# Projections with the split activations side by side as one moving operand, and a prologue by channel tiles

## The chip, the cores and the metric

The kernel runs on one core of a Trainium2 chip. Five engines share the work: TensorE (PE in the profile; its weight loads are listed apart as PEld), VectorE (DVE), ScalarE (ACT), GpSimd (POOL) and SyncE (SP), which issues most transfers from memory. Each engine executes its own queue in order; engines wait for each other on semaphores. The metric is the device time of one execution in microseconds (us). Several executions are timed, and the median counts.

## The reference

A trunk of two layers works on 256 tokens of 1024 channels, in float32. Each layer is, cut to what matters:

```python
h = rms_norm(x, norm_mix_pre)
proj = h @ w_in                      # 1024 -> 1536 + 4*512 + 32 + 512 + 3*1024
u_hy, q, k, v, g_out, gate_lr, u_pool, gate_logits = split(proj)
y_hy   = hyena(u_hy)                 # conv3, then a long convolution by FFT with a filter made by a sine MLP
y_gla  = gla(q, k, v, g_out, gate_lr)  # gated linear attention, 4 heads, both directions
y_pool = pool(u_pool)                # centred means over 2, 4, 8, 16 tokens, 128x128 product per group
gates  = sigmoid(gate_logits)        # 3 x 1024
merged = gates0 * (y_hy @ w_br_hyena) + gates1 * (y_gla @ w_br_gla) + gates2 * (y_pool @ w_br_pool)
x = x + rms_norm(merged @ w_out, norm_mix_post)
h = rms_norm(x, norm_ffn_pre)
a, b = split(h @ ffn_w_up)           # 2 x 2816
y = (gelu(conv3(a)) * b) @ ffn_w_down
x = x + rms_norm(y, norm_ffn_post)
```

## The kernel before

All large products are done in a reduced-precision float format (float32r) by three terms: each operand is split into an upper part (rounded, written by ACT) and a lower part (the rest, a subtraction on DVE), and the product is upper x upper + upper x lower + lower x upper, added up in PSUM. The helper `split` does this for activations, `mm3` issues the three products.

Weights come in chunks of 1 MB (128 partitions x 2048), 71 per layer, through three `raw` buffers that SP's queue fills (`dma_next`). `split_half` splits half a chunk: one ACT instruction (128x1024) and one DVE subtraction. A `unit` is one step of PE's work: it makes sure that its chunk is split, issues its products, runs the pending evictions of earlier units, and then, for each 2.6 us of PE cost, calls `tick` (each running side job, such as the Hyena, attention and pooling jobs, issues its next step) and one or two `filler` splits of later chunks. `ahead` says how many chunks ahead the fillers may go. Between the windows opened by `open_window`, in which PE, DVE and ACT keep the written order, a planner orders the instructions of each engine by priority and a simulated timeline.

Buffers are taken from three pools: `big` (37 of 4 KB per partition), `sml` (9 of 2 KB) and `psm` (8 PSUM banks of 2 KB, 512 columns each). Side jobs wait in `tick` until enough are free (`len(psm.free) < 3`, `len(sml.free) < 3`).

The normalised activations are transposed so that channels lie on partitions: `xt` holds 8 channel tiles (k = 0 to 7) of 256 tokens. Before the change, it is four `big` buffers: two for the upper parts and two for the lower parts, with four channel tiles each. `transposes` fills them from two PSUM banks, one half of the channels at a time.

Two forms of projection use `xt`. `chunk_x_stationary` loads a piece of x as the stationary operand and streams 512 weight columns past it (values and output gates of the attention, branch gates, the output projection, and the first 1024 columns of the b half of the up projection). `two_ftiles` loads weights and streams the 256 tokens: it makes two tiles of 128 output channels (f = 0, 1) in the two halves of one PSUM bank, by two units of 24 products, 256 columns each. Its `post` reads the bank. In a layer's mixer there are 12 calls: eight channel-pair projections whose post is `hy_post` (a conv3 per tile, on ACT and then twice on DVE) or `qk_post` (two DVE instructions of 128x512), in the order x1, v, x1, v, x0, x0, q, q, then two `pool_post` (a copy by ACT, then a side job), then two for k. The up projection has 18 calls: 11 for a (`a_post`: conv3 for both tiles, then gelu on ACT) and 7 for b (`b_post`: a multiplication, and the split for the down projection). The mixer of layer 0 also hosts that layer's filter job (`filt`); the filter of layer 1 runs within the up projections of layer 0.

The prologue is written out by hand. x is loaded in three transfers (two halves of the first 128 tokens, then the second 128), with the first weight chunk between them in two transfers of 512 KB; `grow`, the first norm's gains, goes on SP's queue ahead of the weights. `squares(t)` gives the sums for row tile t on ACT and DVE, `scaled` multiplies by the reciprocal root, `turned` transposes on PE into four PSUM banks, `gained(t, half, ps, banks)` applies the gains and splits. `upper(k)` and `lower(k)` split a quarter of the first chunk. The second row tile's transposes are issued by `second` from within the first unit.

Of the kernel before, what the change touches and what calls it, by code (L numbers as in the profile page):

```python
# [18 lines left out]
P = 128  # L19
# [62 lines left out]


@with_exitstack
def trunk(ctx: ExitStack, tc: tile.TileContext, a: dict, out: bass.AP):
# [5 lines left out]
    big = Slots(spool, "b", 37, 4096)  # L91
    sml = Slots(spool, "s", 9, 2048)
    psm = Slots(ppool, "p", 8, 2048)
# [76 lines left out]
    grow = cpool.tile([8, P], F32, name="grow")  # L170
    nc.sync.dma_start(grow[:], a["gains"][0, 0].rearrange("(k c) -> k c", c=P))

# [10 lines left out]
    def dma_next(parts=1, between=None):  # L183
        n = state["dma"]
        if n >= len(order):
            return
        kind, c = order[n]
        w = 2048 if kind == "w" else 512
        r = wpool.tile([P, w], F32, tag="raw", name=f"raw{n}")
        src = a["wts"][c] if kind == "w" else a["lrw"][c]  # L190
        if kind == "w" and c % NCHUNK in PAIRED:
            side = (c % NCHUNK - 16) % 3
            for m in range(2):
                src = a["wts"][c - side + m][:, side * 1024:(side + 1) * 1024].rearrange("p (k c) -> p k c", c=256)
                nc.sync.dma_start(r[:].rearrange("p (k c) -> p k c", c=512)[:, :, m * 256:(m + 1) * 256], src)
            parts = 0
        for m in range(parts):
            s = slice(m * w // parts, (m + 1) * w // parts)
            nc.sync.dma_start(r[:, s], src[:, s])
            if between is not None and m == 0:  # L200
                between()
        raws[n] = r
        state["dma"] = n + 1
# [50 lines left out]

    dma_next(2, lambda: load_x(1, [slice(0, DM)]))
    dma_next(2)
# [112 lines left out]
    def transposes(h, t, xth, xtl):  # L369
# [7 lines left out]
        for half in range(2):  # L377
            split(xth[half][:, :, s], xtl[half][:, :, s], ps[half][:])
        psm.put(*ps)
# [87 lines left out]
    def filt(i, kf):  # L467
# [102 lines left out]
    def ftile(n, xt, f, o, width=256, kn=8):  # L570
        xth, xtl = xt
        for k in range(kn):
            h, l = weights(n, k * width + f * P, P)
            mm3(o, h, l, xth[k // 4][:, k % 4, :], xtl[k // 4][:, k % 4, :], k == 0, k == kn - 1)

    def two_ftiles(n, xt, post):
        ps = psm.get([P, 2, L])
        unit([n], lambda: ftile(n, xt, 0, ps[:, 0, :]))

        def fin():  # L580
            post(ps)
            psm.put(ps)

        unit([n], lambda: ftile(n, xt, 1, ps[:, 1, :]), fin, free=n)

# [5 lines left out]
    def layer(i, xt, chains):  # L591
# [152 lines left out]

        two_ftiles(take(), xt, hy_post("x1", 0))
        two_ftiles(take(), xt, hy_post("v", 0))
        two_ftiles(take(), xt, hy_post("x1", 2))
        two_ftiles(take(), xt, hy_post("v", 2))

# [137 lines left out]
        x0 = room([P, 4, L])  # L887
        two_ftiles(take(), xt, hy_post("x0", 0))
        f_hy = start(hyena())
        two_ftiles(take(), xt, hy_post("x0", 2))  # L890

# [3 lines left out]
        big.put(g2)  # L895
        two_ftiles(take(), xt, qk_post(eb, 0, float(P ** -0.5)))
        handles["x0"] = True
        two_ftiles(take(), xt, qk_post(eb, 1, float(P ** -0.5)))

# [64 lines left out]

        two_ftiles(take(), xt, pool_post(0))
        two_ftiles(take(), xt, pool_post(2))
        for pair in range(2):
            two_ftiles(take(), xt, qk_post(enb, pair, None))

# [96 lines left out]
        def branch(b, ready):  # L1066
            for half in range(2):
# [15 lines left out]
                if b == 2 and half == 1:  # L1083
                    flush()
                    big.put(*xt[0], *xt[1])
                if b == 2:
# [52 lines left out]
        for t in range(2):  # L1139
            banks = [psm.get([P, 512]) for _ in range(2)]  # L1140
            ready = [False, False]
            ch2.append(start(post_norm(t, banks, g_post_t, g_pre2, *xt2, ready), LIFT))
            for c in range(4):
# [101 lines left out]
        for at, (t, c) in enumerate(seq):  # L1245
            if not done_first and c == 1:
                done_first = True
                flush()
                big.put(*xt2[0], *xt2[1])
                xt3 = xt_alloc() if not last else (None, None)  # L1250

            def fin(t=t):
                ch3.append(start(post_norm(t, banks[t], g_post2, None if last else g_cur["pre"], *xt3), LIFT))
            oldest = min(cc for _, cc in seq[at:])
# [5 lines left out]
        if last:  # L1260
            ready = [False, False]
            ch3.append(start(post_norm(1, banks[1], g_post2, None, *xt3, ready)))
            tail = [(half, c) for half in range(2) for c in range(11 - LEAD, 11)]
# [243 lines left out]
```

## Time and profile before

| what | value |
|---|---|
| time, median of 3 runs | 886.82 us (885.36 to 887.30) |
| profiled execution, its own time | 885.61 us |
| its span, first to last instruction | 883.8 us |
| granted TensorE clock | 0.998 of full speed |
| PE busy | 871.4 us, 5381 products |
| DVE busy | 635.8 us, 925 instructions |
| ACT busy | 511.8 us, 809 instructions |
| memory traffic | 163.46 MB, mean 185 GB/s |

The profiled execution is one run with the hardware profiler on; its own time is a little longer than the span, which begins at the first instruction and ends with the last. Busy time is the time in which an engine had at least one instruction in work. Lines such as L120 or L111 are helpers that record all products or all DVE subtractions, so instructions are told apart by their tiles: `b<-raw,b` is the lower part of a weight split, `p<-b,b` a product of two large buffers, `s<-p` a read of a PSUM bank into a small buffer. In a row of a timeline the columns are start and length in us, engine, line, operation, tiles, shapes, count, and in brackets the idle time before and what ended it.

### The profile page before, as it was taken

The page shows a single profiled execution, that of the slowest core. Times are in us where ns is not written, and L with a number is a line of the kernel's source. Part 1 is how long each engine was busy: PE and PEld are TensorE (multiplying, and loading weights), DVE is VectorE, ACT ScalarE, POOL GpSimd, SP SyncE. Part 2 cuts the span into 40 slices and gives each one's busy share as a digit, 9 for nine tenths or more (in the row PEclk, how much of TensorE's full clock was granted, in tenths as well). Part 3 has the DMA queues.
Part 4 walks back from the last instruction along what each step waited for, and adds up shares of the span by engine and source line. Part 5 has one row for each costly group of instructions (what it writes and reads, how often), then busy time and mean ns, then how long its engine had stood idle before and what let it go on. Part 6 is the DMA issues. An engine that isn't in the chain of part 4 may idle for free.

```text
span 883.8 us, 13488 instructions
## 1 busy us (share of the span) xinstructions
PE 871.4 (99%) x5381; PEld 782.4 (89%) x5381; DVE 635.8 (72%) x925; ACT 511.8 (58%) x809; POOL 37.9 (4%) x86
## 2 busy tenths in 40 slices
PE   8999999999999999999999999999999999999996
PEld 6899987888888999998889999888888899999885
DVE  6899989766586798665288989876755967776612
ACT  6778757555365776554267855864543665555501
POOL 3000100000010000000010000000000000000000
PEclk9999999999999999999999999999999999999999
DMA  8863625746546436466349453455752674455501
GB/s 287 325 233 131 215 96 190 240 145 238 191 159 246 143 134 248 149 221 224 121 136 349 161 164 131 153 195 179 279 184 78 239 281 144 168 170 207 195 1 48
DMA packets 48143, 163.46 MB, mean 185 GB/s; under 512 B 3410, under 2 KB 29157, under 8 KB 33232
## 3 DMA queue, kind: packets, MB, share of 16 engines
q1 hardware_dynamic: 44080, 151.70, 48.9%
q0 software_dynamic: 4000, 10.90, 3.8%
q8 instruction: 42, 0.69, 0.3%
q14 instruction: 21, 0.17, 0.1%
HBM read 161.54 MB, written 1.05 MB: 184 GB/s over the span
## 4 chain that ended last, share of the span: by engine, by line
PE 95%; DVE 2%; DMA 1%; ACT 1%; issue 0%; SPq 0%; DVEq 0%; POOLq 0%; ACTq 0%
PE p L120 93%; DMA raw<-in_wts 1%; DVE b L111 1%; ACT b L106 1%; PE p L374 1%; PE p L1059 0%; PE p L1204 0%; PE p L775 0%; PE p L1021 0%; PE p L876 0%; DVE s L111 0%; PE p L1294 0%; SPq L159 0%; DVE x L114 0%; DVEq L1503 0%
## 5 line engine op out<-in xcount | busy, mean ns | idle before, releaser
L120 PE MATMUL p<-b,b 128*128 128x256 f32 (+2 forms) x5022 | 840.1, 328 | 4.0 <-DVE b L111 2.3
L120 PEld LDWEIGHTS p<-b,b 128*128 128x128 f32 x5022 | 739.8, 190 | 86.6 <-DVE b L111 3.7
L111 DVE TENSOR_TENSOR b<-raw,b 128x1024 fp32r<-128x1024 f32 (+2 forms) x288 | 342.3, 1208 | 114.1 <-ACT b L106 59.6
L106 ACT ACTIVATE b<-raw 128x1024 fp32r<-128x1024 f32 (+2 forms) x290 | 292.2, 1041 | 161.2 <-PE p L120 127.4
L111 DVE TENSOR_TENSOR b<-p,b 128x512 f32<-128x512 f32 (+2 forms) x72 | 45.8, 655 | 66.1 <-ACT s L106 44.6
L106 ACT ACTIVATE b<-p 128x512 f32<-128x512 f32 (+3 forms) x90 | 50.0, 571 | 64.2 <-PE p L120 38.7
L106 ACT ACTIVATE s<-p 128x256 f32<-128x256 f32 (+3 forms) x50 | 20.3, 415 | 69.0 <-PE p L120 68.7
L114 DVE SCALAR_TENSOR_TENSOR s<-p,vec,s 128x255 f32<-128x255 f32 x104 | 49.4, 479 | 6.5 <-ACT s L106 5.5
L106 ACT ACTIVATE s<-p,vec 128x256 f32<-128x256 f32 x52 | 28.8, 557 | 18.1 <-DVE s L114 15.5
L106 ACT ACTIVATE s<-s 128x512 f32<-128x512 f32 (+6 forms) x54 | 28.9, 535 | 11.5 <-DVE s L111 5.6
L111 DVE TENSOR_TENSOR b<-s,b 128x512 fp32r<-128x512 f32 (+1 forms) x42 | 28.6, 686 | 6.0 <-ACT b L106 6.0
L106 ACT ACTIVATE b<-s 128x512 fp32r<-128x512 f32 x38 | 23.5, 625 | 9.2 <-DVE s L111 9.1
L111 DVE TENSOR_TENSOR b<-b,b 128x512 f32<-128x512 f32 (+4 forms) x28 | 22.4, 802 | 3.6 <-ACT b L106 3.1
L111 DVE TENSOR_TENSOR b<-b,p 128x512 f32<-128x512 f32 x24 | 16.2, 683 | 7.7 <-PE p L120 7.3
L111 DVE TENSOR_TENSOR s<-s,p 128x512 f32<-128x512 f32 x22 | 15.0, 684 | 8.4 <-ACT s L106 8.0
L106 ACT ACTIVATE b<-b,s 128x128 f32<-128x128 f32 x64 | 20.5, 392 | 0.4 <-DVE s L700 0.4
L114 DVE SCALAR_TENSOR_TENSOR b<-p,vec,b 128x255 f32<-128x255 f32 (+1 forms) x40 | 19.1, 478 | 0.4 <-ACT b L106 0.3
L387 POOL TENSOR_TENSOR rstd<-mse,mhalf 128x1 f32<-128x1 f32 x16 | 9.3, 581 | 210.5 <-DVE mse L117 210.5
L106 ACT ACTIVATE b<-p,vec 128x256 f32<-128x256 f32 (+1 forms) x24 | 12.6, 527 | 9.0 <-PE p L120 7.1
L106 ACT ACTIVATE b<-b 1x512 f32<-1x512 f32 (+3 forms) x16 | 12.5, 783 | 4.2 <-DVE b L111 4.1
L106 ACT ACTIVATE s<-x 128x512 f32<-128x512 f32 x12 | 7.6, 634 | 11.6 <-DVE x L114 11.4
L111 DVE TENSOR_TENSOR s<-b,b 128x512 f32<-128x512 f32 x20 | 13.1, 685 | 1.5 <-PE p L120 1.4
(108 smaller groups left out, 310.7 us busy)
## 6 DMA issues: line engine op xcount, KB each, us to landing
raw<-in_wts SPq DMA_DIRECT2D x116, 1024.0 KB, 4.8
raw<-in_wts SPq DMA_DIRECT2D x52, 512.0 KB, 5.3
b<-in_gains POOLq DMA_DIRECT2D x7, 512.0 KB, 4.5
b<-in_dft POOLq DMA_DIRECT2D x4, 512.0 KB, 6.9
b<-in_gw POOLq DMA_DIRECT2D x2, 512.0 KB, 5.5
b<-in_fw POOLq DMA_DIRECT2D x2, 512.0 KB, 7.3
b<-in_decay POOLq DMA_DIRECT2D x2, 512.0 KB, 7.3
out<-x SPq DMA_DIRECT2D x4, 256.0 KB, 2.0
```

The lines of the kernel that those rows point to most:

```text
L106: ins = nc.scalar.activation(o, i, func, **kw)
L111: nc.vector.tensor_tensor(out=o, in0=x, in1=y, op=op)
L114: nc.vector.scalar_tensor_tensor(out=o, in0=x, scalar=s, in1=y, op0=op0, op1=op1)
L120: ins = nc.tensor.matmul(o, w, x, start=start, stop=stop).ins
L374: nc.tensor.transpose(ps[k // 4][:, k % 4, :], h[:, k * P:(k + 1) * P], ident[:])
L387: nc.gpsimd.tensor_tensor(out=r[:], in0=e[:], in1=mhalf[:, 0:1], op=ALU.pow)
```

## The change

Five things change.

1. `xt` is laid out by channel tiles: four buffers, each with two channel tiles, and for each of them the upper part and then the lower part, 512 columns in a row. `Part` gives the old view of it (upper or lower part of a channel tile), so that other users are the same. `transposes` writes each half of the channels in two pieces.
2. `two_ftiles` has a wide form, used in layer 1's mixer (`i > 0`) and in both layers' up projections. It takes one small buffer and two banks, one bank for each of the two output tiles. A first unit issues, for both tiles, 8 products each of the upper weights with 512 columns (upper x into the bank's first half, lower x into its second half); a second unit issues 8 products each of the lower weights with the 256 columns of the upper x, into the first half. Then ACT copies the second half to the small buffer and DVE adds the first half to it, for each tile, and `post` reads the small buffer in place of a PSUM bank. The costs that the units give are 3.6 and 1.9 in place of 2.6 and 2.6.
3. `sml` has 10 buffers.
4. In the prologue, the first weight chunk comes in four transfers, with x's second row tile after two of them; `grow` is issued from ACT's queue; `squares(1)` goes ahead of the second part of `gained(0, 0, ...)`, and `scaled(1, ...)` ahead of `lower(3)`.
5. In the filter job, the upper part of the last filter weight (`w3h`) is issued on ACT behind `hs`, the upper part of the sines.

```diff
+class Part:
+    def __init__(self, tiles, m):
+        self.tiles, self.m = tiles, m
+    def __getitem__(self, at):
+        _, k, s = at
+        return self.tiles[k // 2][:, k % 2, self.m, s]
+    def two(self, j, s):
+        return self.tiles[j][:, :, self.m, s]
...
-    sml = Slots(spool, "s", 9, 2048)
+    sml = Slots(spool, "s", 10, 2048)
...
-    nc.sync.dma_start(grow[:], a["gains"][0, 0].rearrange("(k c) -> k c", c=P))
+    nc.scalar.dma_start(grow[:], a["gains"][0, 0].rearrange("(k c) -> k c", c=P))
...
-            if between is not None and m == 0:
+            if between is not None and 2 * m + 2 == parts:
...
-    dma_next(2, lambda: load_x(1, [slice(0, DM)]))
+    dma_next(4, lambda: load_x(1, [slice(0, DM)]))
...
         for half in range(2):
-            split(xth[half][:, :, s], xtl[half][:, :, s], ps[half][:])
+            for j in range(2):
+                split(xth[half].two(j, s), xtl[half].two(j, s), ps[half][:, 2 * j:2 * j + 2, :])
...
-        act(hs[:], h2[:])
+        with tc.issue_after(nc.scalar.activation(hs[:], h2[:], AF.Copy).ins):
+            act(w3h[:], kf["w3"][:])
         tt(hs[64:P, :], h2[64:P, :], f32(hs[64:P, :]), ALU.subtract)
-        act(w3h[:], kf["w3"][:])
         tt(w3l[:], kf["w3"][:], f32(w3h[:]), ALU.subtract)
...
     def xt_alloc():
-        return ([big.get([P, 4, L], F32R) for _ in range(2)], [big.get([P, 4, L], F32R) for _ in range(2)])
+        ts = [big.get([P, 2, 2, L], F32R) for _ in range(4)]
+        return (*([Part(ts[2 * j:2 * j + 2], m) for j in range(2)] for m in range(2)), ts)
...
+    def ftiles_wide(n, xt, banks, lows):
+        for f, o in enumerate(banks):
+            for k in range(8):
+                h, l = weights(n, k * 256 + f * P, P)
+                x = xt[2][k // 2][:, k % 2]
+                if lows:
+                    mm(o[:, 0, :], l, x[:, 0, :], False, k == 7)
+                else:
+                    mm(o[:], h, x, k == 0, False)
...
-    def two_ftiles(n, xt, post):
+    def two_ftiles(n, xt, post, wide=True):
+        if not wide:
...
+        while not sml.free:
+            tick()
...
+        tmp = sml.get([P, 2, L])
+        banks = [psm.get([P, 2, L]) for _ in range(2)]
+        def fin():
+            for f, ps in enumerate(banks):
+                act(tmp[:, f, :], ps[:, 1, :])
+                tt(tmp[:, f, :], tmp[:, f, :], ps[:, 0, :], ALU.add)
+            psm.put(*banks)
+            post(tmp)
+            sml.put(tmp)
+        unit([n], lambda: ftiles_wide(n, xt, banks, False), cost=3.6)
+        unit([n], lambda: ftiles_wide(n, xt, banks, True), fin, cost=1.9, free=n)
...
-        two_ftiles(take(), xt, hy_post("x1", 0))
+        two_ftiles(take(), xt, hy_post("x1", 0), i > 0)
...
     lower(1)
-    gained(0, 0, ps0, (1,))
     h1, ss1 = squares(1)
     r1 = rstd_mean(ss1)
-    for k in (2, 3):
-        upper(k)
-        lower(k)
+    gained(0, 0, ps0, (1,))
+    upper(2)
+    lower(2)
+    upper(3)
     scaled(1, h1, r1)
+    lower(3)
```

All 12 calls of `two_ftiles` in the mixer get `i > 0`; the calls of the up projections are left as they are written, so they take the wide form.

More of the change, by code (lines that the diff above doesn't have):

```diff
@@ L570, in ftile @@
     def ftile(n, xt, f, o, width=256, kn=8):
-        xth, xtl = xt
+        xth, xtl = xt[:2]
         for k in range(kn):
             h, l = weights(n, k * width + f * P, P)
-            mm3(o, h, l, xth[k // 4][:, k % 4, :], xtl[k // 4][:, k % 4, :], k == 0, k == kn - 1)
-    def two_ftiles(n, xt, post):
-        ps = psm.get([P, 2, L])
-        unit([n], lambda: ftile(n, xt, 0, ps[:, 0, :]))
-        def fin():
-            post(ps)
-            psm.put(ps)
-        unit([n], lambda: ftile(n, xt, 1, ps[:, 1, :]), fin, free=n)
+            s = slice(0, L)
+            mm3(o, h, l, xth[k // 4][:, k % 4, s], xtl[k // 4][:, k % 4, s], k == 0, k == kn - 1)
+    def ftiles_wide(n, xt, banks, lows):
[9 more added lines that the diff above has]
+        if not wide:
+            ps = psm.get([P, 2, L])
+            unit([n], lambda: ftile(n, xt, 0, ps[:, 0, :]))
+            def fin():
+                post(ps)
+                psm.put(ps)
+            unit([n], lambda: ftile(n, xt, 1, ps[:, 1, :]), fin, free=n)
+            return
+        c = 0
+        while not sml.free:
+            tick()
+            c += 1
+            assert c < 500, "no room"
+        tmp = sml.get([P, 2, L])
+        banks = [psm.get([P, 2, L]) for _ in range(2)]
+        def fin():
+            for f, ps in enumerate(banks):
[6 more added lines that the diff above has]
+        unit([n], lambda: ftiles_wide(n, xt, banks, True), fin, cost=1.9, free=n)
     def conv3(o, ps, i, col):
@@ L743, in hy_post @@
             return post
-        two_ftiles(take(), xt, hy_post("x1", 0))
-        two_ftiles(take(), xt, hy_post("v", 0))
-        two_ftiles(take(), xt, hy_post("x1", 2))
-        two_ftiles(take(), xt, hy_post("v", 2))
+        two_ftiles(take(), xt, hy_post("x1", 0), i > 0)
+        two_ftiles(take(), xt, hy_post("v", 0), i > 0)
+        two_ftiles(take(), xt, hy_post("x1", 2), i > 0)
+        two_ftiles(take(), xt, hy_post("v", 2), i > 0)
         def qk_post(dst, pair, scale):
@@ L887, in layer @@
         x0 = room([P, 4, L])
-        two_ftiles(take(), xt, hy_post("x0", 0))
+        two_ftiles(take(), xt, hy_post("x0", 0), i > 0)
         f_hy = start(hyena())
-        two_ftiles(take(), xt, hy_post("x0", 2))
+        two_ftiles(take(), xt, hy_post("x0", 2), i > 0)
         drain(f_dec, *gates_ready)
@@ L895, in layer @@
         big.put(g2)
-        two_ftiles(take(), xt, qk_post(eb, 0, float(P ** -0.5)))
+        two_ftiles(take(), xt, qk_post(eb, 0, float(P ** -0.5)), i > 0)
         handles["x0"] = True
-        two_ftiles(take(), xt, qk_post(eb, 1, float(P ** -0.5)))
+        two_ftiles(take(), xt, qk_post(eb, 1, float(P ** -0.5)), i > 0)
         pw = sml.get([P, 4, P])
@@ L963, in pool_post @@
             return post
-        two_ftiles(take(), xt, pool_post(0))
-        two_ftiles(take(), xt, pool_post(2))
+        two_ftiles(take(), xt, pool_post(0), i > 0)
+        two_ftiles(take(), xt, pool_post(2), i > 0)
         for pair in range(2):
-            two_ftiles(take(), xt, qk_post(enb, pair, None))
+            two_ftiles(take(), xt, qk_post(enb, pair, None), i > 0)
         y_gl = {}
@@ L1084, in branch @@
                     flush()
-                    big.put(*xt[0], *xt[1])
+                    big.put(*xt[2])
                 if b == 2:
@@ L1141, in layer @@
             ready = [False, False]
-            ch2.append(start(post_norm(t, banks, g_post_t, g_pre2, *xt2, ready), LIFT))
+            ch2.append(start(post_norm(t, banks, g_post_t, g_pre2, *xt2[:2], ready), LIFT))
             for c in range(4):
@@ L1248, in layer @@
                 flush()
-                big.put(*xt2[0], *xt2[1])
+                big.put(*xt2[2])
                 xt3 = xt_alloc() if not last else (None, None)
             def fin(t=t):
-                ch3.append(start(post_norm(t, banks[t], g_post2, None if last else g_cur["pre"], *xt3), LIFT))
+                ch3.append(start(post_norm(t, banks[t], g_post2, None if last else g_cur["pre"], *xt3[:2]), LIFT))
             oldest = min(cc for _, cc in seq[at:])
@@ L1261, in layer @@
             ready = [False, False]
-            ch3.append(start(post_norm(1, banks[1], g_post2, None, *xt3, ready)))
+            ch3.append(start(post_norm(1, banks[1], g_post2, None, *xt3[:2], ready)))
             tail = [(half, c) for half in range(2) for c in range(11 - LEAD, 11)]
```

## The prediction

> **What bounds the kernel now.** I read the page first, then who waited for whom on PE, then the stages.
>
> ```profile
> span 883.8 us, 13488 instructions
> PE 871.4 (99%) x5381; PEld 782.4 (89%) x5381; DVE 635.8 (72%) x925; ACT 511.8 (58%) x809; POOL 37.9 (4%) x86
> PE 95%; DVE 2%; DMA 1%; ACT 1%; issue 0%; SPq 0%; DVEq 0%; POOLq 0%; ACTq 0%
> ```
>
> ```profile
> PE p L120 <- DVE b L111: 2.3, 2, 1.8
> PE p L120 <- ACT b L106: 1.8, 2, 1.4
> ```
>
> PE is busy 99% of the span, is 95% of the chain that ended last, and its longest wait on another engine is 1.8 us. A busy PE is not a PE at its peak, so the rate comes from the chain in order of time (start, length, what). Two rows hold products of a single kind: 48 products of 512 columns between two sets of transposes, and 144 of 256 columns (three pairs of up projections).
>
> ```profile
> 254.18 10.90 PE p L120 x48
> ...
> 735.62 17.28 PE p L120 x144
> ```
>
> 10.90/48 = 0.2271 us per 512-column product, 17.28/144 = 0.1200 us per 256-column one. The 256 extra columns cost 0.1071 us, so 0.013 us of each product does not depend on its width. Each has its own weight load in both stages (PE and PEld both count 5381). So the time is the number of PE instructions and their columns, and fewer instructions for the same columns shorten it, unless DVE or ACT come late. Where that could be is in the stages (length, busy time of each engine, clock):
>
> ```profile
> 60.00:91.00 31.00, 31.00 (x246) 30.02 (x245) 30.90 (x63) 26.60 (x55) 1.87 (x6) 1.00 0.31 121
> 91.00:116.00 25.00, 25.00 (x199) 24.46 (x199) 22.63 (x39) 15.59 (x35) 2.51 (x8) 1.00 0.59 190
> 269.50:386.00 116.50, 116.50 (x904) 112.26 (x903) 89.01 (x129) 70.86 (x96) 2.68 (x5) 1.00 0.53 189
> 477.00:552.00 75.00, 75.00 (x615) 74.43 (x614) 65.75 (x118) 49.82 (x99) 3.81 (x13) 1.00 0.52 175
> 552.00:570.00 18.00, 18.00 (x92) 15.19 (x91) 16.63 (x28) 15.93 (x26) 0.00 (x0) 1.00 0.37 110
> 701.60:817.00 115.40, 115.40 (x925) 113.59 (x925) 80.31 (x104) 66.12 (x86) 0.57 (x1) 1.00 0.55 195
> ```
>
> Layer 0's mixer (60 to 116) has DVE at 30.90 of 31 us, and behind it stands the one long PE stall of the trace, 1.78 us before this row:
>
> ```profile
> 136.41 5.96 PE L120 MATMUL p<-b,b 128*128 128x512 f32 x25 [1.78 <-DVE b L111]
> ```
>
> The change leaves that mixer narrow. Layer 1's mixer (477 to 552) has DVE at 65.75 of 75; the up projections (269.5 to 386 and 701.6 to 817) at 89.01 of 116.5 and 80.31 of 115.4.
>
> **The change, part by part.** Wide products. A narrow two_ftiles is 2 x 8 x 3 = 48 products of 256 columns: 48 x 0.1200 = 5.76 us. A wide one is 16 of 512 and 16 of 256: 16 x 0.2271 + 16 x 0.1200 = 5.55 us. The gain is 0.206 us per call. Calls: 18 in layer 0's up projections, 12 in layer 1's mixer, 18 in its up projections, 48 in all: 3.7 + 2.5 + 3.7 = 9.9 us, and 768 PE instructions fewer. The wide row is taken from a stage that streams weights past x, but what counts is columns and one load per product, and these are the same.
>
> The Trainium skill, "TensorE: Matmul & The Clock Gate", section "Back-to-back issue gap", speaks against this: it gives N/2.4 + 2.5 ns between warm products, so only 2.5 ns of each would be saved, an estimate of 768 x 2.5 ns = 1.9 us in place of 9.9. The two rows above differ from it (120 ns for its 109, 227 for its 216), at a granted clock of 1.00, so the measured 13 ns decides.
>
> What a wide call adds, from groups with shapes kept apart (busy, mean ns of one):
>
> ```profile
> L106 ACT ACTIVATE s<-p 128x256 f32<-128x256 f32 (+3 forms) x50 | 20.3, 415 | 69.0 <-PE p L120 68.7
> L106 ACT ACTIVATE s<-p 128x256 f32<-128x256 f32 x16 | 5.8, 383 | 3.8 <-PE p L120 3.6
> L111 DVE TENSOR_TENSOR b<-p,b 128x256 fp32r<-128x256 f32 x8 | 3.4, 421 | 5.4 <-ACT b L106 5.4
> L114 DVE SCALAR_TENSOR_TENSOR s<-p,vec,s 128x255 f32<-128x255 f32 x104 | 49.4, 479 | 6.5 <-ACT s L106 5.5
> L114 DVE SCALAR_TENSOR_TENSOR s<-b,b 128x256 f32<-128x256 f32 x8 | 3.2, 423 | 0.0
> ```
>
> Per call two ACT copies out of PSUM, 2 x 0.383 = 0.77 us, and two DVE additions, 2 x 0.421 = 0.84 us. The convolutions after them read SBUF instead of PSUM, which for a DVE instruction of this size is 0.423 instead of 0.479: 4 x 0.056 = 0.22 us back in each of the 28 calls that convolve. By stage, DVE:
>
> - Up projections of one layer: 18 x 0.84 - 11 x 0.22 = +12.7 us. Idle there: 116.5 - 89.0 = 27.5 and 115.4 - 80.3 = 35.1, less the 3.7 us by which the stage shrinks. It fits; cost nothing. ACT (+13.9 on 70.9 of 116.5) fits too. If a whole add and copy of every call stood in the open, it would be 18 x 1.6 us a layer.
> - Layer 1's mixer: 12 x 0.84 - 6 x 0.22 = +8.8 us on 65.75, in 75 - 2.5 = 72.5 us. DVE is wanted for 74.5: it becomes as full as in layer 0's mixer. Which idle time can be used, from the waits of DVE between 474 and 575 (total, times, longest):
>
> ```profile
> DVE b L111 <- PE p L120: 5.2, 5, 1.9
> DVE b L111 <- ACT b L106: 4.9, 5, 1.3
> DVE b L114 <- PE p L120: 1.4, 1, 1.4
> ```
>
> Waits for PE, 6.6 us, vanish when DVE is the later one; waits for ACT stay. 8.8 + 2.5 - 6.6 = 4.7 us of lateness at most reach the branch products behind 552, where DVE has 1.4 us free in 18. Weights are split some chunks ahead, so the lower bound is 0. Between 0 and 4.7 I take 2.0, nearest to the 1.8 us that the like stage of layer 0 pays. What is late then is a weight's low part, or the pooling branch, whose last piece ends just as PE gets to it already now:
>
> ```profile
> 572.53 0.48 DVE L114 SCALAR_TENSOR_TENSOR b<-p,vec,b 128x256 fp32r<-128x256 f32 x1
> 572.61 6.63 PE L120 MATMUL p<-b,b 128*128 128x512 f32 x28
> ```
>
> Banks. A wide call holds two PSUM banks where a narrow one held one, and a buffer of the small pool, of which there is one more. When side work is asked for between units, the call before has given its own back, so 6 of 8 banks are free instead of 7; side work asks for 3 or 4. Nothing, at least while one or two side jobs hold banks.
>
> Layout. Transposes split each half in two pieces: per call of it ACT 4 x 0.380 for 2 x 0.593, DVE 4 x 0.421 for 2 x 0.686, +0.3 us on each, six calls.
>
> ```profile
> L106 ACT ACTIVATE b<-p 128x512 fp32r<-128x512 f32 x24 | 13.5, 593 | 21.8 <-PE p L1059 19.3 <-PE p L374 2.4
> L106 ACT ACTIVATE b<-p 128x256 fp32r<-128x256 f32 x8 | 3.0, 380 | 3.7 <-PE p L1021 3.7
> L111 DVE TENSOR_TENSOR b<-p,b 128x512 fp32r<-128x512 f32 x24 | 15.8, 686 | 11.7 <-ACT b L106 11.7
> ```
>
> PE still has products of the other row tile when these run (the 48 of the row at 254.18, of which half do not need them). Nothing; up to 1.2 us in all if that cover is short.
>
> Filter: w3's upper part now goes behind the sines on ACT, and its DVE subtraction (128x1024; 1.22 us like those of the weights) with it. In layer 0 that moves from an early gap of DVE toward the stretch at 30.90 of 31; the 2.4 us idle in 91 to 116 can take it. 0 to 1.2 us, I take 0.4. The saturated stretch may also swallow part of what the prologue gains.
>
> Prologue (start, length, engine; then a transfer's size and time from issue to landing):
>
> ```profile
> 1.65 0.37 SPq L171 DMA_DIRECT2D grow<-in_gains  x1
> 2.46 0.43 SPq L159 DMA_DIRECT2D x<-in_x  x1
> 3.61 0.63 ACT L106 ACTIVATE b<-x 128x512 f32<-128x512 f32 x1 [1.59 <-DMA x<-in_x]
> 5.95 0.72 ACT L106 ACTIVATE b<-x,rstd 128x512 f32<-128x512 f32 x1 [1.62 <-POOL rstd L387]
> 8.04 0.63 ACT L106 ACTIVATE b<-raw 128x512 fp32r<-128x512 f32 x1 [1.37 <-DMA raw<-in_wts]
> 10.09 0.64 ACT L106 ACTIVATE b<-x 128x512 f32<-128x512 f32 x1
> 11.88 1.28 DVE L111 TENSOR_TENSOR b<-raw,b 128x512 fp32r<-128x512 f32 x2
> ```
>
> ```profile
> x<-in_x SPq DMA_DIRECT2D x1, 512.0 KB, 6.8
> ```
>
> SP saves the issue of grow, 0.37, and pays two more for quarters; ACT issues grow inside its 1.59 us wait. ACT waits 1.37 us for 512 KB of weights; a quarter of the chunk can end that wait. Then squares(1), moved one group ahead, meets the landing of x's second half, 2.46 + 6.8 = 9.3 at the earliest, so it starts 0.8 us before its present 10.09. One of the two subtractions of the last row (128x512, 0.64 each) leaves the path to the second transposes. I take -0.8, from -1.2 to +0.4 (one issue more, nothing landing earlier).
>
> Sum: -9.9 (products) -0.8 (prologue) +2.0 (layer 1's branches) +0.4 (filter) = -8.3 us. The profiled execution took 885.61 us, 1.8 over its span: 877.3. It lies 1.2 us under the median of the runs shown, 886.82, which gives 878.5; I forecast 878.0. The terms' ends give 885.6 - 9.9 - 1.2 = 874.5 and 885.6 - 9.9 + 0.4 + 4.7 + 1.2 + 1.2 = 883.2.
>
> **Rivals.** (1) All cover holds and there is no stall: 885.6 - 10.7 = 874.9. For it: splits run ahead; against: DVE wanted for 74.5 of 72.5 us.
> (2) Lateness at its bound in layer 1 and some in the layer 0 stretch: +4.7 +1.2 and no prologue gain: 881.6 to 883. For it: the pooling rows, with 0.08 us between them.
> (3) The width-independent part does not go away, by the rule cited beside the products: were it so, with 2.0 us in place of 9.9 the sum is -0.4 and the time 885 to 886. Against: the two PE rows.
> (4) Slower: the posts serialise. Copy, addition, convolution hand over between ACT and DVE in order, and if each pair of copy and addition keeps DVE for 0.80 instead of 0.42 us, a call takes 1.6 us of it: 12 x 1.6 - 1.3 = 17.9 us in the mixer against 6.6 usable, 11.3 + 2.5 = 13.8 us of PE waits, 2.5 more in layer 0's up projections (28.8 - 2.5 against 27.5 - 3.7), 16 against 10.7 gained: about 891. It decides once PE waits exceed 10.7 us. For it: in-order queues; against: only 4.9 us of DVE waits for ACT in those 101 us, since splits lie between.
>
> **How the numbers follow.** Forecast 0.62, (1) 0.06, (2) 0.17, (3) 0.05, (4) 0.10. Less than 0.2% (1.8 us) cannot be told from no change here. Faster: 0.62 + 0.06 + 0.17 = 0.85; same: (3), 0.05; slower: (4), 0.10. The range runs from (1) to just past (2), 874 to 884.5, and leaves out (3) and (4), 0.15.
>
> **What would show it.** PE x4613 (5381 - 768), 512-column products still 227 ns apart; DVE near 636 + 34 + 2 us, ACT near 512 + 37 + 2. Second transposes of the prologue at 12.3 to 12.8. Waits of PE on DVE or ACT of 2 to 4 us in all, most of it in layer 1 behind the mixer. The forecast is wrong if a wide product takes more than 227 ns, or if PE waits pass 5 us.

## The result and the profile after

| | before | after |
|---|---|---|
| median of 6 runs each, side by side | 886.09 us (884.21 to 887.40) | 891.15 us (889.21 to 892.07) |
| profiled execution: own time, span | 885.61, 883.8 us | 891.14, 889.4 us |
| mean granted TensorE clock | 0.998 | 0.993 |

The ratio is 1.0055 (95% interval 1.0043 to 1.0068): the change makes the kernel slower by some 5 us, where 8 to 9 us less were forecast. First the profile's page of the kernel after: span, busy times, and the shares of the chain that ended last.

```profile
span 889.4 us, 12162 instructions
PE 870.8 (98%) x4613; PEld 745.6 (84%) x4613; DVE 665.7 (75%) x1033; ACT 541.1 (61%) x917; POOL 38.5 (4%) x86
PE 88%; DVE 5%; ACT 3%; DMA 2%; issue 1%; POOL 0%; SPq 0%; DVEq 0%; POOLq 0%; ACTq 0%
```

There are 768 products fewer, as counted, and yet PE's share of the chain falls from 95% to 88%. The waits of PE on the other engines (total, times, longest) had been 2.3 and 1.8 us; after:

```profile
PE p L133 <- ACT b L119: 8.0, 7, 2.0
PE p L133 <- DVE b L124: 1.4, 3, 0.8
...
PE p L387 <- DVE b L127: 1.0, 2, 0.7
PE p L824 <- ACT b L119: 0.3, 1, 0.3
```

Where they lie is in the chain in order of time (start, length, what). The first row is the start of the steady stream of products, the last a piece that holds three wide calls:

```profile
12.70 61.13 PE p L133 x413
...
119.88 5.50 DVE b L124 x9
130.71 5.60 DMA raw<-in_wts
...
140.88 4.61 DMA raw<-in_wts
...
557.35 1.58 ACT b L119 x2
558.98 7.94 PE p L133 x26
...
744.29 16.70 PE p L133 x96
```

Three calls are 48 products of 512 and 48 of 256 columns: 48 x 0.2271 + 48 x 0.1200 = 16.66 us by the prediction's prices, and 16.70 is measured. So the wide products give what they promised. In the chain of before the same stream starts later:

```profile
14.68 62.03 PE p L120 x417
```

That is 14.68 - 12.70 = 1.98 us gained in the prologue. Gains of 9.9 + 2.0 = 11.9 us are there, and 5.6 us more span; so some 17.5 us were lost. To place them I take, for each product behind 14 us, the distance to the start of the next, less 0.227, 0.120 or 0.109 us for 512, 256 or 128 columns, and add these up by stretches of the span. That is my own sum over PE's rows, in us; the runs e2 to e17 come below. Each column is one execution, and executions of one kernel differ: that of e9 is 1.9 us under its median and that of e6 1.0 us over, and a lower granted clock goes with a longer span.

| stretch (us of the span) | before | after | e2 | e5 | e6 | e8 | e9 | e13 | e14 | e17 |
|---|---|---|---|---|---|---|---|---|---|---|
| 14 to 62 | 1.2 | 1.1 | 1.2 | 2.5 | 1.1 | 1.1 | 1.1 | 1.1 | 1.1 | 1.1 |
| 62 to 94, layer 0's mixer | 0.1 | 4.3 | 0.0 | 0.1 | 6.6 | 5.6 | 0.1 | 5.6 | 5.4 | 0.1 |
| 128 to 158, layer 0 behind the mixer | 2.2 | 7.4 | 4.4 | 2.0 | 1.3 | 1.2 | 2.4 | 1.2 | 1.2 | 2.0 |
| 255 to 475, turn and up projections | 1.2 | 3.2 | 1.2 | 4.0 | 2.9 | 3.3 | 4.5 | 2.9 | 2.8 | 2.8 |
| 547 to 570, layer 1 behind the mixer | 0.2 | 5.6 | 0.2 | 0.1 | 6.2 | 0.2 | 0.2 | 2.2 | 5.9 | 2.4 |
| all behind 14 us | 6.2 | 24.1 | 9.3 | 10.9 | 20.4 | 13.7 | 10.6 | 15.5 | 18.7 | 10.8 |

24.1 - 6.2 = 17.9 us are lost: 4.2 near 75 us, 5.2 behind layer 0's mixer, 2.0 at and after the turn to the up projections, 5.4 behind layer 1's mixer. Four places; the sum of the prediction had 2.0 us for the last and 0.4 us for the filter's order, which touches the first two. The stages of the kernel after, in the columns of the prediction's stage rows:

```profile
70.00:85.00 15.00, 13.07 (x85) 11.89 (x85) 14.64 (x33) 11.78 (x30) 1.21 (x3) 0.89 0.53 193
126.00:155.00 29.00, 25.10 (x102) 19.01 (x101) 20.70 (x36) 20.55 (x35) 0.56 (x1) 0.94 0.46 147
545.00:575.00 30.00, 26.73 (x138) 22.26 (x137) 29.80 (x55) 21.11 (x37) 0.12 (x1) 0.94 0.30 96
```

And of before:

```profile
70.00:85.00 15.00, 15.00 (x116) 14.48 (x115) 15.00 (x31) 11.61 (x27) 1.36 (x5) 1.00 0.51 193
126.00:155.00 29.00, 27.22 (x123) 22.24 (x122) 25.48 (x39) 21.63 (x32) 0.04 (x1) 1.00 0.54 184
545.00:575.00 30.00, 30.00 (x176) 26.42 (x174) 27.00 (x45) 21.76 (x35) 0.00 (x0) 1.00 0.55 175
```

### The profile page after: what moved, and what is told of

It is laid out like the page before. It is cut to its first block, busy times and chain, and to the rows that moved or that the text cites. A ratio compares the mean times of both kernels' runs of the same rounds, so it can differ in the third digit from the quotient of the medians.

```text
span 889.4 us, 12162 instructions
## 1 busy us (share of the span) xinstructions
PE 870.8 (98%) x4613; PEld 745.6 (84%) x4613; DVE 665.7 (75%) x1033; ACT 541.1 (61%) x917; POOL 38.5 (4%) x86
## 4 chain that ended last, share of the span: by engine, by line
PE 88%; DVE 5%; ACT 3%; DMA 2%; issue 1%; POOL 0%; SPq 0%; DVEq 0%; POOLq 0%; ACTq 0%
PE p L133 86%; DVE b L124 3%; ACT b L119 2%; DMA raw<-in_wts 2%; ACT s L119 1%; DVE b L127 1%; DVE x L127 1%; PE p L387 0%; PE p L1253 0%; PE p L1108 0%; DVE s L124 0%; POOL rstd L401 0%; PE p L1070 0%; PE p L824 0%; PE p L925 0%
## 5 line engine op out<-in xcount | busy, mean ns | idle before, releaser
L133 PE MATMUL p<-b,b 128*128 128x512 f32 (+2 forms) x4254 | 838.7, 357 | 9.7 <-ACT b L119 8.0
L133 PEld LDWEIGHTS p<-b,b 128*128 128x128 f32 x4254 | 702.5, 190 | 127.1 <-ACT b L119 10.8
L119 ACT ACTIVATE s<-p 128x256 f32<-128x256 f32 (+3 forms) x146 | 54.8, 388 | 86.0 <-PE p L133 85.7
L124 DVE TENSOR_TENSOR s<-s,p 128x256 f32<-128x256 f32 (+1 forms) x104 | 43.1, 435 | 5.3 <-ACT s L119 5.2
L127 DVE SCALAR_TENSOR_TENSOR s<-s,vec,s 128x255 f32<-128x255 f32 x96 | 43.8, 479 | 4.2 <-ACT s L119 3.9
L119 ACT ACTIVATE s<-s 128x512 f32<-128x512 f32 (+5 forms) x52 | 28.4, 546 | 20.8 <-DVE s L127 16.0
L119 ACT ACTIVATE b<-s 128x512 fp32r<-128x512 f32 (+1 forms) x40 | 24.8, 625 | 11.8 <-DVE s L124 11.8
L119 ACT ACTIVATE s<-s,vec 128x256 f32<-128x256 f32 x48 | 27.0, 591 | 4.2 <-DVE s L124 4.2
L124 DVE TENSOR_TENSOR s<-s,s 128x512 f32<-128x512 f32 (+2 forms) x30 | 20.1, 669 | 4.4 <-ACT s L499 2.3
L133 PE MATMUL p<-b,s 128*128 128x128 f32 (+1 forms) x80 | 13.4, 298 | 0.0
```

The costliest lines, as they stand in the source:

```text
L119: ins = nc.scalar.activation(o, i, func, **kw)
L124: nc.vector.tensor_tensor(out=o, in0=x, in1=y, op=op)
L127: nc.vector.scalar_tensor_tensor(out=o, in0=x, scalar=s, in1=y, op0=op0, op1=op1)
L133: ins = nc.tensor.matmul(o, w, x, start=start, stop=stop).ins
```

## The experiments

Each run stands beside runs of the kernel before on the same chip (medians 885.25 to 885.83 us); ratios are to those, with their 95% interval. Single letters in the texts on record are names of theories.

### One part alone, and all parts but the wide products

e1: the change with `two_ftiles` narrow everywhere.

```diff
     def two_ftiles(n, xt, post, wide=True):
+        wide = False
```

> The changed kernel with every call of two_ftiles narrow: the prologue, the filter order, the tenth small buffer and the layout by channel tiles stay. Theory A (the loss sits in the narrow mixer of layer 0 and has nothing to do with the wide products): the PE waits of 9 to 10 us between 55 and 155 us stay, and without the 9.9 us that wide products save the time is 893 to 900. Theory B (the wide products and their copies bring the loss, through DVE and ACT): the waits in layer 0 go, and the time is 884 to 888.

Measured: 894.06 us, 1.0103 (1.0083 to 1.0122). Without any wide product the loss is larger than with them: 8.7 us come from the parts around them. By the sum of the table e1 pays 2.8, 6.2 and 2.8 us at the first three places and 0.1 behind layer 1's mixer: the loss there comes with the wide calls, the others come without them.

e2: the kernel before with one line of the change.

```diff
-    sml = Slots(spool, "s", 9, 2048)
+    sml = Slots(spool, "s", 10, 2048)
```

> The kernel before with ten small buffers in place of nine, nothing else. Theory S (the tenth buffer lets the filter and decay-gate side jobs of layer 0 run sooner, and their DVE work is put ahead of the weight splits): PE waits of 5 us or more in layer 0's mixer, time 890 or more. Theory not S: within 1 us of before, 885 to 887.

Measured: 889.60 us, 1.0050 (1.0035 to 1.0065). One more small buffer alone costs 4.3 us. Its waits of PE, and its stage behind layer 0's mixer:

```profile
PE p L120 <- ACT b L106: 4.5, 4, 2.0
PE p L120 <- DVE b L111: 1.3, 3, 0.6
...
126.00:155.00 29.00, 25.67 (x112) 19.67 (x111) 21.00 (x33) 20.87 (x36) 0.55 (x1) 1.00 0.44 147
```

Side jobs wait in `tick` for three free small buffers. As I read the program, with one more they step sooner and put their instructions into the written order of ACT and DVE ahead of weight splits; between 110 and 126 us DVE has 28 instructions here and 23 before, ACT 6 and 10, and the DMA share is 0.12 and 0.22. How many low parts of weights DVE makes between 90 and 160 us (count, then first and last start), first before, then here:

```profile
L111 DVE TENSOR_TENSOR b<-raw,b x22: 1215/1219/1226, 90.1 to 157.0; 128x1024 fp32r<-128x1024 f32 x22
```

```profile
L111 DVE TENSOR_TENSOR b<-raw,b x19: 1211/1218/1226, 90.0 to 157.5; 128x1024 fp32r<-128x1024 f32 x19
```

Three fewer. A raw buffer comes free only after its split, so SP loads the next chunk later, and then ACT waits for memory with nothing left to split (last row; two rows of ACT in this run):

```profile
133.51 2.01 ACT L106 ACTIVATE b<-raw 128x1024 fp32r<-128x1024 f32 x2 [0.99 <-DMA raw<-in_wts]
...
152.23 1.06 ACT L106 ACTIVATE b<-raw 128x1024 fp32r<-128x1024 f32 x1 [5.55 <-DMA raw<-in_wts]
```

The chain of the kernel after shows the same links: nine DVE pieces from 119.88, then transfers of weights at 130.71 and 140.88.

e3: before, with the filter's order alone (part 5 of the change). e4: before, with the prologue alone (part 4).

> The kernel before with the filter edit alone (w3's upper part behind the sines). Theory F (1.2 us of DVE and the latency of the filter move into the saturated stretch of layer 0): 887 to 892, PE waits behind 60 us. Theory not F: 885 to 887.5, as the prediction had it (+0.4).

> The kernel before with the prologue edit alone. Theory P (layer 0 is bound by DVE up to 137 us, so PE starts 2 us sooner and waits 2 us more there): 885.5 to 887. The prediction: the start is kept, 885.3. If the sooner start were kept whole, with the 2 us that the changed kernel's trace shows (12.7 for 14.7): 884.

Measured: 885.35 us, 0.9997 (0.9987 to 1.0006), and 885.12 us, 0.9998 (0.9985 to 1.0010). Neither moves the median alone. In e4 the stream begins 1.6 us sooner (at 13.08), and PE's one long wait is the one that before has as well, 1.78 us there:

```profile
135.02 5.28 PE L120 MATMUL p<-b,b 128*128 128x512 f32 x22 [1.79 <-DVE b L111]
```

So this trace keeps the gain (span 881.9 us, before 883.8). With a granted clock of 0.998 or more the spans of e4 are 881.7 to 881.9 us, in three executions of ten, and those of before beside it 882.7 to 883.9, in eleven of nineteen: the gain is there, and the median loses it because the clock is lower in more of e4's executions. Why it is lower in them is not shown.

e5: before, with the layout by channel tiles and the transposes split in two pieces (part 1), `two_ftiles` narrow.

> The kernel before with the layout by channel tiles alone (four buffers, transposes split in two pieces per half; nine small buffers, all products narrow). The prediction: hidden, 885 to 886.5. Theory X (the pieces lengthen the turns between the output projection and the up projection, and the layout changes the order in layer 0): PE waits of 0.8 us near 270 us and 0.4 near 704 us, as in the run without wide products, and a wait of 2 us near 75 us; 887 to 889.

Measured: 889.35 us, 1.0034 (1.0021 to 1.0047); by the medians 4.1 us, by the ratio 3.0. The larger part of the loss is at the turns (2.8 us of extra spacing between 255 and 475, 2.2 of them at the first); 1.3 us more lie between 14 and 62 us, where the granted clock of this execution is 0.76 from 14 to 20 us and 1.00 in before. At the first turn the second set of transposes waits behind the 48 products (rows of PE in this run, then before):

```profile
254.67 11.14 PE L133 MATMUL p<-b,b 128*128 128x512 f32 x48
267.60 1.32 PE L387 MATMUL p<-ident,b 128*128 128x128 f32 x8 [1.80 <-DVE b L127]
```

```profile
253.94 11.15 PE L120 MATMUL p<-b,b 128*128 128x512 f32 x48
264.92 1.04 PE L374 MATMUL p<-ident,b 128*128 128x128 f32 x8
```

What is late is the scaling of the next row tile on DVE. Counted from the start of the 48 products it comes 12.13 us behind them here (at 266.80) and 9.38 in before (at 263.32), 2.75 us later. The first tile's splits stand ahead of it. The four small subtractions, with waits between the pieces, end 4.13 us behind that start where the two large ones ended at 2.92: 1.2 us. Last subtraction of DVE here, and then before:

```profile
258.38 0.42 DVE L124 TENSOR_TENSOR b<-p,b 128x256 fp32r<-128x256 f32 x1 [0.45 <-ACT b L119]
```

```profile
255.58 1.28 DVE L111 TENSOR_TENSOR b<-p,b 128x512 fp32r<-128x512 f32 x2
```

The other 1.5 us are on ACT, between the two squares of the norm. There the upper part of layer 1's `w3` (`b<-b`, 128x1024), which waits for its transfer, stands between them. ACT here, and then before:

```profile
261.72 0.63 ACT L119 ACTIVATE s<-x 128x512 f32<-128x512 f32 x1 [1.84 <-DVE x L127]
...
263.01 1.06 ACT L119 ACTIVATE b<-b 128x1024 fp32r<-128x1024 f32 x1 [0.57 <-DMA b<-in_fw]
263.98 0.61 ACT L119 ACTIVATE s<-x 128x512 f32<-128x512 f32 x1
```

```profile
259.71 0.63 ACT L106 ACTIVATE s<-x 128x512 f32<-128x512 f32 x1 [2.01 <-DVE x L114]
...
260.47 0.63 ACT L106 ACTIVATE s<-x 128x512 f32<-128x512 f32 x1
```

Part 5 of the change moves this instruction. Among the runs with the new layout, the five without part 5 (e5, e9, e11, e15, e16) have it between the squares, and their second transposes wait 1.3 to 2.0 us; the kernel after and the nine others have the squares side by side, and wait 0.3 to 0.7 us. In e6:

```profile
269.22 1.32 PE L388 MATMUL p<-ident,b 128*128 128x128 f32 x8 [0.32 <-DVE b L128]
```

So layout and filter order share a cost too: the small pieces alone cost little at the turn once `w3` is out of the way.

### The tenth buffer inside the change

e6: the change, with one small buffer held back until layer 0's up projections.

```diff
+    kept = [sml.free.pop()]
...
+        if kept:
+            sml.free.append(kept.pop())
```

> The changed kernel with the tenth small buffer held back until layer 0's up projections begin. Theory S (in the changed kernel, too, the tenth buffer costs the 4 to 5 us of layer 0): 885.5 to 887, PE waits between 120 and 155 us at most 2.5 us in all. If the layer 0 loss has another cause in the changed kernel: 889 or more.

Measured: 886.69 us, 1.0009 (1.0000 to 1.0018): 4.5 us of the loss against after are gone by the medians of two chips; counted from the runs of before beside each (5.06 and 1.44 us above them) it is 3.6 us. Between 128 and 158 us the extra spacing falls from 7.4 to 1.3 us; near 75 us it grows to 6.6, and layer 1's 6 us stay (stage row below).

```profile
545.00:575.00 30.00, 26.22 (x128) 21.74 (x127) 29.34 (x53) 22.11 (x41) 0.12 (x1) 0.94 0.39 124
```

### Layer 1's mixer

e7: as e6, and the two DVE additions of each of the 12 wide calls in layer 1's mixer left out; what is left out of the computation is the term of lower x and upper weights there. e12: as e6, with unit costs of 3.4 and 1.8 in place of 3.6 and 1.9, so that side jobs are stepped less often.

```diff
+                if add:
+                    tt(tmp[:, f, :], tmp[:, f, :], ps[:, 1, :], ALU.add)
```

```diff
-        unit([n], lambda: ftiles_wide(n, xt, banks, False), cost=3.6)
+        unit([n], lambda: ftiles_wide(n, xt, banks, False), cost=3.4)
```

> As the run with one buffer held back, with the 24 DVE additions of layer 1's mixer left out (ACT copies the bank's first half, and the upper x times lower term is dropped there, so the output is off). Theory D (DVE's added 10 us in that mixer make the waits of 5 us behind it, near 555 to 563 us): these waits fall under 1 us and the run is 4 to 6 us faster than with the additions. Theory O (the order in which work was planned, or ACT's copies, makes them): they stay above 3 us, and less than 2 us are gained.

> The changed kernel with one buffer held back in layer 0 and the costs that the two units of a wide call give lowered from 3.6 and 1.9 to 3.4 and 1.8, so that side jobs step twice per call as before. Theory T (a wide call lets the side jobs step too often for its PE time, so the inverse transform of Hyena comes up in PE's queue before DVE and ACT have split its operand): the waits of 4 us between 550 and 556 fall by half or more, and the run takes 884 to 885.5 against 886.7. If stepping is not the cause: the waits stay over 3 us.

Measured: 887.42 us, 1.0019 (1.0009 to 1.0029), and 889.62 us, 1.0043 (1.0029 to 1.0057). Theory D of e7 and theory T of e12 fall; that PE's wait stays and little is gained was e7's other theory. In e12 the extra spacing behind layer 1's mixer grows, to 8.1 us. The stage of e7:

```profile
545.00:575.00 30.00, 26.48 (x126) 21.70 (x125) 25.64 (x45) 20.41 (x37) 0.12 (x1) 0.94 0.45 151
```

DVE has 3.7 us less to do than in e6 and PE waits as long. It is not DVE's load that sets this wait.

e13: as e6, and the last four calls of layer 1's mixer (two `pool_post`, two for k) narrow. e14: as e6, and the first eight narrow.

```diff
-        two_ftiles(take(), xt, pool_post(0), i > 0)
+        two_ftiles(take(), xt, pool_post(0), False)
```

> The change with the tenth small buffer held until layer 0's up projections, and in layer 1's mixer only the first eight calls wide (x1, v, x1, v, x0, x0, q, q); the last four (two pooling, two k) narrow. Theory E (the last calls' posts, which stand on DVE and ACT just ahead of the Hyena job's last splits, make those late): the waits of PE between 545 and 565 us fall from 4.7 us to under 1.5, and the time to 884 or less. Theory B (the first calls push the Hyena job or the splits back already): waits of 3 us or more stay, 886 to 888.

> As the run before, the other way round: the first eight calls of layer 1's mixer narrow and the last four wide. Theory E: waits between 545 and 565 us of 3 us or more, 886 to 888. Theory B: waits under 1.5 us, 884 or less. If both of these runs show small waits, DVE's total is what counts and not the place; if both show large ones, any wide call there turns the plan.

Measured: 884.54 us, 0.9991 (0.9979 to 1.0002), and 889.30 us, 1.0042 (1.0026 to 1.0058). Both times lie above what was expected (884 or less, 886 to 888), the second by more than 1 us; why is not shown.

The last four calls carry most of the cost: wide, they leave 5.9 us of extra spacing, narrow 2.2. With all twelve narrow it is 0.2 (e8), so 2.0 us come with the first eight. The waits of PE themselves fall in e13 to 0.4 us up to 565 us, as expected, with one of 1.07 us at 570. PE's rows show what is late. In e6, behind the last projections:

```profile
553.49 0.50 PE L134 MATMUL p<-b,b 128*128 128x512 f32 x1 [1.63 <-ACT b L120]
555.73 1.65 PE L134 MATMUL p<-b,b 128*128 128x512 f32 x3 [1.74 <-ACT b L120]
```

By the order of the program these products of 512 columns are Hyena's inverse transform; they wait for the upper parts of its input, which ACT writes at 552.79 and 555.06:

```profile
552.79 0.64 ACT L120 ACTIVATE b<-s 128x512 fp32r<-128x512 f32 x1
554.10 1.06 ACT L120 ACTIVATE b<-raw 128x1024 fp32r<-128x1024 f32 x1 [0.66 <-DMA raw<-in_wts]
555.06 0.61 ACT L120 ACTIVATE b<-s 128x512 fp32r<-128x512 f32 x1
```

In e13 PE has 29 products of 512 columns (6.8 us) at that place, and none of these waits is there. Whether the last four calls' two banks, their shorter time on PE, or the planner's order takes that cover away was not told apart.

### The wait near 75 us, and the wide up projections

e8: the kernel before with layout, prologue, filter order and wide up projections; nine small buffers, layer 1's mixer narrow. e9: e8 without the filter's order. e10: e8 without the prologue. e11: e8 without both.

> The changed kernel with nine small buffers and narrow products in layer 1's mixer, too: wide products in the up projections alone. Theory S and theory D together: no waits in layer 0 beyond those of before and none behind layer 1's mixer, 7.4 us gained by 36 wide calls less about 1.3 us at the turns: 878.5 to 881. If the up projections do not yield their gain: 884 to 886.

> As the run with wide products in the up projections alone and nine buffers, with the filter edit taken back, too. Theory F2 (together with the layout, w3 behind the sines delays the filter's eviction on ACT, and PE waits 3.7 us for its bank near 75 us): that wait goes, and the time is 880 to 881.5 against 884.1. If the wait comes from the prologue or from the layout alone: it stays, 883.5 to 884.5.

> As the run with wide products in the up projections alone and nine buffers, with the prologue edit taken back. Theory F2: the wait near 75 us stays at 2 to 4 us, 884 to 886. Theory P2 (the sooner start makes it): it goes, 880.5 to 882.

> Layout and wide up projections alone, nine buffers, without prologue and filter edits. No wait near 75 us, as in the run with the layout alone; the up projections yield 7.4 us on that run's 889.35: 881 to 883. If the up projections yield less than half of their product sum: 885.5 or more.

| run | prologue | filter order | us | ratio (interval) |
|---|---|---|---|---|
| e8 | yes | yes | 884.11 | 0.9980 (0.9969 to 0.9991) |
| e9 | yes | no | 881.76 | 0.9961 (0.9936 to 0.9985) |
| e10 | no | yes | 882.35 | 0.9954 (0.9939 to 0.9970) |
| e11 | no | no | 883.80 | 0.9972 (0.9957 to 0.9987) |

Against e5, e11 adds wide up projections alone: 889.35 - 883.80 = 5.5 us less, where 7.4 were counted; at a granted clock of 0.998 or more the spans are 887.1 us (two executions of e5) and 879.3 and 879.6 (two of e11), 7.6 us apart, so the missing part goes with the clock. The two edits that leave the median alone make a wait together, on top of the new layout; the pair without the layout was not run. The wait does not decide the medians by itself: e11 has 0.1 us of extra spacing near 75 us, but 4.6 behind layer 0's mixer and 6.0 from 255 to 475, and its interval overlaps that of e8. Row of PE in e8, and ACT's row that ends it:

```profile
78.98 4.39 PE L133 MATMUL p<-b,b 128*128 128x256 f32 x21 [3.58 <-ACT b L119]
```

```profile
78.24 0.69 ACT L119 ACTIVATE b<-p,signs 128x512 f32<-128x512 f32 x1
```

That ACT row reads, and so frees, a PSUM bank of the filter job. In before it came at 74.72, in e9 at 74.66; in e8 fourteen short instructions from 73.74 us on stand ahead of it, and the next products on PE wait for it. How late ACT's row comes does not decide alone: in e17 it comes at 77.99 and in e10 at 80.84, and PE does not wait. What PE's queue has next counts as well; why the planner writes the orders so only when both edits are in was not traced further. The granted clock from 70 to 85 us is 0.89 in e8 and 1.00 in e9, so the 5.5 us of extra spacing between them are more than the 3.58 us of the wait.

e15: e6 without the filter's order, all else of the change in.

> The change with the tenth small buffer held until layer 0's up projections and without the filter's reordering; everything else of the change is in, layer 1's mixer wide. If the filter's reordering is needed for the wait near 75 us, that wait (3.7 us with the buffer held) is gone, and the time is about 886.7 - 3 = 883 to 884, with the waits behind layer 1's mixer (4 to 5 us) still there. If it comes without the reordering too, 886 to 887.

Measured: 884.99 us, 0.9993 (0.9976 to 1.0009). The wait near 75 us is gone here too (0.1 us of extra spacing), so the full change needs the reordering for it as well. Behind the mixer of layer 0 the extra spacing rises from 1.3 to 4.0 us, and at the turn the wait is 1.31 us in place of 0.32, so that only 1.7 us of time are won against e6, where 3 were expected.

### A mended version

e16: e13 without the filter's order. e17: e13 without the changed prologue; its edit does not give back the order of before quite, since `gained(0, 0, ps0, (1,))` stands ahead of `upper(1)`, where neither kernel has it.

> The change mended in three places: tenth small buffer held until layer 0's up projections, only the first eight calls of layer 1's mixer wide, no reordering in the filter. If the three costs are separate, the time is that of the run with the last four narrow (884.5) less what the wait near 75 us cost there (3.7 us of extra spacing, of which the run without the reordering gave back 1.7, since 1.1 us came back near 132): 881 to 883.5, and PE has no wait over 1.5 us behind layer 1's mixer.

> The same, but with the filter's reordering and without the changed prologue. If it is the two together that make the wait near 75 us, it is gone here as well; the second transposes stand at 14 us again in place of 12.7. 880.5 to 883.

Measured: 882.68 us, 0.9960 (0.9948 to 0.9973), and 880.23 us, 0.9944 (0.9932 to 0.9956). e17 beats both kernels: 5.6 us less than before, some 11 less than the change as made. Its second transposes stand at 12.83 us, between before (13.48) and after (11.69). e16, with the changed prologue and without the filter's order, pays 4.5 us of extra spacing behind layer 0's mixer and 4.0 from 255 to 475, where e17 pays 2.0 and 2.8. The profile's page of e17:

```profile
span 878.4 us, 12273 instructions
PE 865.3 (99%) x4677; PEld 744.5 (85%) x4677; DVE 663.2 (76%) x1025; ACT 539.6 (61%) x909; POOL 38.3 (4%) x86
```

By the count it has 44 wide calls: 44 x 0.206 = 9.1 us gained, 10.8 - 6.2 = 4.6 us of extra spacing paid, 4.5 expected, and 883.8 - 878.4 = 5.4 us of span measured.

## Why the prediction was wrong

**The step that failed.** "Banks. A wide call holds two PSUM banks ... and a buffer of the small pool, of which there is one more ... Nothing". I asked whether side work would find fewer banks in the calls that change. What I did not ask was what one more small buffer does everywhere else: it lets the side jobs of layer 0's mixer, which is narrow as before, step sooner. Alone it costs 4.3 us (e2), in the change 3.6 to 4.5 (e6). The rows for it were in the prediction: DVE at 30.90 of 31 us there, and the one long stall behind it. A resource that throttles side work in a full stage is not free to give. It is not the only one: with the buffer held back the change still takes 886.69 us, above the 884.5 where the range ended, so the terms below failed as well.

**Layout, "Nothing; up to 1.2 us".** Alone 3.0 to 4.1 us (e5), in the change 2.0 at and behind the turns. Instructions were priced rightly (0.3 us per call); the cover was not. The 48 products at the turn hide the splits themselves, but not the next row tile's scaling, for which PE's next transposes wait 1.80 us in e5. The pieces are 1.2 us of its lateness; the rest is layer 1's `w3` on ACT.

**Filter, "0 to 1.2 us", and prologue, "-0.8".** Each edit alone leaves the median where it was (e3, e4). The prologue's own part was better than forecast: second transposes at 11.69 in place of 12.3 to 12.8, the stream 2.0 us sooner. That "the saturated stretch may also swallow part of what the prologue gains" is not what e4's trace shows: the wait behind that stretch is as long as before. What the prediction did not have is that both edits together bring the bank's wait near 75 us (5.5 us of extra spacing, e8 against e9), and that the filter's order saves some 1 to 1.6 us at the turn (e15 against e6, e9 against e8), where the prediction did not have it. I summed edits that share one written order as if they were independent.

**Layer 1's branches, "+2.0", 0 to 4.7.** 5.4 us, beyond the bound. The bound came from DVE's load; e7 takes that load away and the wait stays. The load was too low besides: the convolutions were to give 0.22 us per call back by reading the small buffer, at 0.423 us in place of 0.479, but they take 0.479 still, so that the 0.423 belonged to another form of the instruction. Group of the kernel after:

```profile
L127 DVE SCALAR_TENSOR_TENSOR s<-s,vec,s 128x255 f32<-128x255 f32 x96 | 43.8, 479 | 4.2 <-ACT s L119 3.9
```

Without that credit the bound would have been 6.0, and the 5.4 would have lain inside it by luck. Neither a weight's low part nor the pooling branch was the main thing late, but Hyena's inverse transform, whose operand's upper parts ACT wrote late; the last four calls bring most of it (e13, e14).

**What held.** PE x4613; products at 227 and 120 ns, so 9.9 us gained; up projections "cost nothing": behind the turns, from 290 to 460 us and from 710 us on, no product of the kernel after starts more than 0.2 us late. DVE 665.7 us (672 forecast), ACT 541.1 (551); DVE's total came near in spite of the wrong credit, because the lengths of its instructions add up to 41.0 us more than before and its busy time to 29.9 (they overlap).

**The rivals.** (4) gave about 891, which the median met by luck, not by its mechanism: additions did not take 0.80 us of DVE. The group in the kernel after (busy, mean ns of one):

```profile
L124 DVE TENSOR_TENSOR s<-s,p 128x256 f32<-128x256 f32 x96 | 37.9, 414 | 4.1 <-ACT s L119 4.1
```

The waits quoted above make 10.7 us in all, where before had 4.1, and the prediction's own sign of being wrong was more than 5; the lower clock behind them (below) and smaller gaps did the rest, and none of it lies in the up projections, where (4) put a part. (1) and (2) needed a gain and fell with the time; (3) fell with the 16.70 us row. The chance of 0.10 for slower was too small because all rivals looked for the loss inside the wide calls.

## What to carry to other kernels

Before a buffer is added to a pool that side jobs wait on, ask which stages those jobs share with work that sets the end, and hold the buffer back until these are past. Where one planner writes the order of several engines, edits of order do not add up: run them alone and in pairs. And where PE is the bound at 99%, look for every product that now comes sooner than its operands do: here a gain of 12 us was given back at four places.

## What was unexpected of the hardware

Short waits of PE can cost more than themselves: behind some of them the granted clock falls to half for a while. Windows of the kernel after behind three of its waits (the third number from the end of a row is the clock):

```profile
78.00:82.00 4.00, 4.00 (x24) 4.00 (x23) 3.72 (x9) 4.00 (x11) 0.54 (x1) 0.59 0.23 66
...
150.00:154.00 4.00, 3.77 (x10) 2.92 (x10) 0.91 (x2) 0.00 (x0) 0.00 (x0) 0.57 0.68 216
...
560.00:564.00 4.00, 4.00 (x11) 2.80 (x10) 4.00 (x8) 1.12 (x3) 0.00 (x0) 0.57 0.00 0
```

In these stretches products of 512 columns stand 0.427 us apart in place of 0.227, and products of 256 columns 0.213 in place of 0.120. The row of PE at 150 us:

```profile
150.36 8.01 PE L133 MATMUL p<-b,b 128*128 128x512 f32 x27 [0.23 <-DVE b L124]
```

27 x 0.227, and 0.2 for the end of the last, would be 6.3 us; 1.7 more are paid, behind waits of 2.02 and 0.23 us. Over the three places it is some 4.6 of the 17.9 us lost (15 products of 256 columns by 0.093, and 16 of 512 by 0.2). The single wait of 1.78 us in before was followed by no such stretch. The Trainium skill, "TensorE: Matmul & The Clock Gate", Part 1, says that the clock passes half of its pulses after an idle window of about 3.4 us that runs free of the kernel. Half the rate agrees with 0.427 us for 512 columns, and (1 - 0.57) x 4.00 / 0.5 = 3.4 us at half the rate fit in the last two windows, an estimate from their rows; but no single wait of PE in the kernel after was longer than 2.02 us. Nor do the waits decide alone. In e2 the same pair, 1.99 us at 146.21 and 0.23 at 147.47, is followed by a clock of 1.00, and in e9 so are single waits of 1.90 and 1.96 us; in e11 a single wait of 1.86 us at 267.69 is followed by this window:

```profile
268.00:272.00 4.00, 4.00 (x16) 3.08 (x14) 4.00 (x5) 1.30 (x3) 0.00 (x0) 0.59 0.37 96
```

What decides was not shown here.
